# A layer's kernel with 128 series of products of zeros ahead of its first stage

## The chip, the cores and the metric

The kernel runs on one core of one Trainium2 chip. The metric is the device time of one execution in microseconds (us), lower is better. Two runs of the kernel before took 1088.96 and 1090.29 us; the median is 1089.62 us. One further execution was recorded by the hardware profiler. All rows of the profile come from that one.

## The reference

The reference computes one inference step of one layer (D = 1024) for a prompt of 512 tokens and a group of 8 x 8 sample tokens that share the weights. Cut to what matters here:

```python
u = _rms(x) * g_pre_mix
proj = u @ w_in                       # one projection: z, xbc, dt, q, k, v, gates, og
xbc, conv_new = causal_conv(xbc, conv_buf, conv_w, conv_b)
y_ssd, h_new = ssd_scan(silu(xbc) ...)          # 16 heads
h_ml, c_new, n_new, m_new = mlstm_scan(q, k, v, i_pre, logf, ...)   # 4 heads
x = x + _rms(concat(y_ssd, h_ml) @ w_out) * g_post_mix
x = x + _rms(cross_attention(_rms(x) * g_pre_x, mem_k, mem_v) @ w_xo) * g_post_x
f = (silu(u @ w_gate) * (u @ w_up)) @ w_down    # u = _rms(x) * g_pre_ffn
x = x + _rms(f) * g_post_ffn
```

All inputs and outputs are float32. Nothing in the reference answers to the products that the change adds: their operands are zeros, and nobody reads their result.

## The kernel before

The 576 tokens (512 of the prompt, 64 samples) lie along the free dimension of the tiles, the features along the 128 partitions, eight blocks of 128 deep. A float32 matrix product is made of three products of float32r parts: weights high by input high, weights high by input low, weights low by input high. Each part of the inputs is 576 columns wide and is taken in two pieces: 256 and 320 columns (`HALVES`) in the projections, 288 and 288 (`EHALVES`) in the output of the cross attention and in most of the feed-forward part. So a unit of weights, 128x1024, gives eight blocks, and per block and piece three products with 128x128 weights; each of them loads its weights anew (PEld in the profile) while the product ahead still runs.

Weights come by DMA in units of 512 KB into one of two `raw` buffers (L175). ScalarE copies the high part (L180), VectorE or a DMA on GpSimd's queue makes the low part (L184 to L187); there are three buffers for each of the split parts, so a later unit waits until TensorE is done with an earlier one.

The beginning: VectorE clears a small tile `wz` (L300), and TensorE makes 21 products of zeros with it, 256 columns of bfloat16 each, into the bank `ps_warm` (L303), which nobody reads. Meanwhile the input and the first two units of weights arrive in pieces on SP's queue (L304 to L314), ScalarE and VectorE make their high and low parts (L191, L192, L322, L323), and the first stage's products follow block by block (L339 to L341), then those of further units (`gemm`, L202 to L205).

Tiles are taken from pools. `MP` gives one of three PSUM banks by turns. `SL(n, ...)` gives one of the big slots of 576 x 8 floats for each partition; slot 1 has no user until the tile `qk` is made in a later part. Whoever takes a buffer waits for its last reader and writer.

Each engine works off its queue in order. In the first part of the kernel, up to the cross attention, the order of an engine's queue is chosen by a planner: it takes the order of the code as a priority, lets some pieces go earlier (`high_priority`) or behind others (`issue_after`), and goes by the times of a simulated run (`schedule_with_timeline_sim`). In the later part the order is written out by hand (`manual_schedule`, L2035 and L2238).

Of the kernel before, what the change touches and what calls it, by code (L numbers as in the profile page):

```python
# [11 lines left out]
F32 = mybir.dt.float32  # L12
F32R = mybir.dt.float32r
# [6 lines left out]
P = 128  # L20
# [95 lines left out]
def build(nc, tc, ctx, I, O):  # L116
    V, A, G, S, TE = nc.vector, nc.scalar, nc.gpsimd, nc.sync, nc.tensor
    mm = TE.matmul
# [12 lines left out]
    def SL(slot, name, dt=F32, shape=(P, KT, T)):  # L131

        return big.tile(list(shape), dt, name=name, tag="s%d" % slot, bufs=1)
# [5 lines left out]
    def MP(name="m"):  # L139
        return pa.tile([P, 512], F32, name=name, tag="a")  # L140
# [54 lines left out]
    def gemm(ps, units, xh, xl, t0, n, k0=0, k1=None, order=None, late=0):  # L195


        tiles = [(hi[:, j * P:(j + 1) * P], lo[:, j * P:(j + 1) * P]) for hi, lo, nk in units for j in range(nk)]
        order = order or range(len(tiles))
        for i, k in list(enumerate(order))[k0:k1]:  # L200
            (wh, wl), ah, al = tiles[k], xh(k, t0, n), xl(k, t0, n)
            mm(ps, wh, ah, start=i == 0, stop=False)  # L202
            mm(ps, wh, al, start=False, stop=False)  # L203
            for c in range(late) if i == late - 1 else [i] if i >= late else ():
                m = mm(ps, tiles[order[c]][1], xh(order[c], t0, n), start=False, stop=c == len(tiles) - 1)  # L205
        return m
# [94 lines left out]
    psw = MP("ps_warm")  # L301
    for _ in range(NWARM):
        mm(psw[:, 0:256], wz[:, 0:128], wz, start=True, stop=True, skip_group_check=True)  # L303
    S.dma_start(par, I["par"])  # L304

    wi = [[wp.tile([P, 1024], F32R, name=k, tag=k, bufs=3) for k in ("whi", "wlo")] for _ in range(2)]
# [46 lines left out]
    stop = gemm(ps0[2][1], [(*w2, KT)], U, UL, 256, 320, 0, NSS)  # L353
# [12 lines left out]
    stop = gemm(ps0[3][0], [(*w3, KT)], U, UL, 0, 256)  # L366
# [343 lines left out]
    for g in range(2):  # L710
        psb = BP("ps_ls")
        pb3 = psb.rearrange("p (h t) -> p h t", h=8)
        for h in range(8):
            mm(psb[:, h * TS:(h + 1) * TS], sel[:80, 8 * g + h:8 * g + h + 1].to_broadcast([80, P]), cumst[:, TP:T],
               start=h == 0, stop=h == 7, skip_group_check=True)
# [8 lines left out]
        for h in range(8):  # L724
            k, j = h % 2, (8 * g + h) // 2
            mm(psi[64 * k:64 * k + 64, j * TS:(j + 1) * TS], xdts[:, 8 * g + h, :], lm[:, h, :], start=True, stop=True,
               skip_group_check=True)
# [12 lines left out]
    for b in range(4):  # L740
# [3 lines left out]
        for g in range(2):  # L744
            for hb in (1, 0):
# [3 lines left out]
                   start=b == 0, stop=b == 3, skip_group_check=True)  # L749
# [139 lines left out]
    for h in range(4):  # L889
        q, k = qk[:, h, :], qk[:, 4 + h, :]  # L890
# [11 lines left out]
        for c in range(4):  # L902
            mm(pss[:, c * P:(c + 1) * P], k[:, c * P:(c + 1) * P], q[:, c * P:(c + 1) * P], start=True, stop=True,
               skip_group_check=True)
# [39 lines left out]
    for h in range(4):  # L944
        mm(psb[:, h * TS:(h + 1) * TS], sel[:68, h:h + 1].to_broadcast([68, P]), sxst[:, TP:T], start=h == 0, stop=h == 3,
           skip_group_check=True)
# [22 lines left out]
    for hb in range(2):  # L969
# [6 lines left out]
        for b in range(4):  # L976
# [3 lines left out]
            for h in range(4):  # L980
                mm(psn[32 * h:32 * h + 32, 0:257], qpad[:, h, bb, :], c0[:, h, 0:257], start=False, stop=b == 3,
                   skip_group_check=True)
# [241 lines left out]
    x = SL(1, "x1")  # L1224
# [956 lines left out]
    parts = [(c, d) for c in range(2) for d in range(2)]  # L2181
# [172 lines left out]
```

## Time and profile before

| | |
|---|---|
| median of two runs | 1089.62 us |
| the profiled execution's own time | 1087.01 us |
| its span, first to last instruction | 1085.2 us |
| mean granted TensorE clock | 0.998 of full speed |
| matrix products recorded | 8124 |
| TensorE products (PE) busy | 1075.0 us |
| TensorE weight loads (PEld) busy | 1022.1 us |
| VectorE (DVE) busy | 752.4 us |
| ScalarE (ACT) busy | 610.9 us |
| GpSimd (POOL) busy | 228.0 us |

Times in the profile count from the first instruction of the span. PE's records of neighbouring products overlap: a product is recorded from its start until its last column has left the array, so the time that a product takes from TensorE is the distance from its start to the next one's start, and not its recorded length. Weight loads overlap the product ahead. A row of the view of groups reads: line, engine, operation, output and inputs, weights' shape, moving operand's shape, count, then busy time in us, mean length in ns, and the idle time ahead with what ended it. In the order of time a row starts with start and length in us.

### The profile page before, as it was taken

How to read it: one execution, taken by the hardware profiler on the slowest of the kernel's cores; microseconds unless marked ns; L12 is line 12 of the kernel's file. 1: busy time of each engine (PE TensorE's matmuls, PEld its weight loads, DVE VectorE, ACT ScalarE, POOL GpSimd, SP SyncE). 2: the span in 40 equal slices, each digit the busy share in tenths (PEclk: the TensorE clock that was granted, in tenths of full speed). 3: DMA queues.
4: the chain of work that ended last, by engine and by line, in shares of the span. 5: the costliest groups of instructions: out<-in, count | busy, mean ns of one | idle time of the engine just before them, and what ended most of it. 6: DMA issues, size and time to landing. Idle time of an engine off the chain costs nothing.

```text
span 1085.2 us, 20708 instructions
## 1 busy us (share of the span) xinstructions
PE 1075.0 (99%) x8124; PEld 1022.1 (94%) x8124; DVE 752.4 (69%) x1507; ACT 610.9 (56%) x1098; POOL 228.0 (21%) x305
## 2 busy tenths in 40 slices
PE   9999999999999999999999999999999999999997
PEld 9999887778999999999999989999999999999997
DVE  6896785658877775568755546766467887787556
ACT  7867632355654555656555545645566566656653
POOL 1332643313113111000154301100011111111000
PEclk9999999999999999999999999999999999999999
DMA  6775535435654449653458775643486697578532
GB/s 211 179 159 126 161 111 172 165 80 185 190 152 144 110 123 324 226 193 101 152 194 288 271 252 180 239 133 92 135 176 137 159 203 163 117 189 184 125 131 88
DMA packets 58966, 182.29 MB, mean 168 GB/s; under 512 B 6604, under 2 KB 11852, under 8 KB 58356
## 3 DMA queue, kind: packets, MB, share of 16 engines
q1 hardware_dynamic: 42740, 138.06, 38.6%
q0 software_dynamic: 15552, 41.95, 19.6%
q8 instruction: 64, 1.05, 0.4%
q10 hardware_dynamic: 576, 0.95, 0.3%
q14 instruction: 34, 0.28, 0.1%
HBM read 160.28 MB, written 20.65 MB: 167 GB/s over the span
## 4 chain that ended last, share of the span: by engine, by line
PE 86%; DVE 5%; ACT 4%; issue 2%; DMA 2%; POOL 0%; DVEq 0%; SPq 0%; ACTq 0%; POOLq 0%
PE ps_in L203 4%; PE ps_in L202 4%; PE ps_in L205 4%; PE ps_v L815 3%; PE ps_o L205 3%; PE ps_o L203 3%; PE ps_g L1846 3%; PE ps_g L1847 3%; PE ps_o L202 3%; PE ps_u L1847 3%; PE ps_u L1848 3%; PE ps_u L1846 3%; PE ps_g L1848 3%; PE ps_dn L1846 2%; PE ps_dn L1847 2%
## 5 line engine op out<-in xcount | busy, mean ns | idle before, releaser
L202 PE MATMUL ps_in<-uh,whi 128*128 128x320 f32 (+1 forms) x544 | 162.9, 300 | 0.5 <-DVE cb L451 0.5
L205 PE MATMUL ps_in<-uh,wlo 128*128 128x320 f32 (+1 forms) x544 | 162.3, 299 | 0.3 <-DMA wlo<-win 0.3
L203 PE MATMUL ps_in<-ul,whi 128*128 128x320 f32 (+1 forms) x544 | 161.8, 298 | 0.0
L180 ACT CAST whi<-raw 128x1024 fp32r<-128x1024 f32 (+1 forms) x104 | 105.2, 1013 | 100.0 <-PE ps_in L203 25.9
L187 DVE TENSOR_TENSOR wlo<-raw,whi 128x512 fp32r<-128x512 f32 (+1 forms) x96 | 93.7, 978 | 75.1 <-ACT whi L180 74.0
L202 PEld LDWEIGHTS ps_in<-uh,whi 128*128 128x128 f32 x544 | 102.8, 189 | 3.3 <-issue 1.7
L205 PEld LDWEIGHTS ps_in<-uh,wlo 128*128 128x128 f32 x544 | 102.3, 188 | 1.5 <-DMA wlo<-win 0.5
L203 PEld LDWEIGHTS ps_in<-ul,whi 128*128 128x128 f32 x544 | 102.4, 188 | 0.6
L185 POOL DMA_DIRECT2D wlo<-win x32 | 27.8, 869 | 80.7 <-ACT wlo L184 70.0
L1847 PE MATMUL ps_g<-b,whi 128*128 128x288 f32 x144 | 42.5, 295 | 0.0
L1846 PE MATMUL ps_g<-b,whi 128*128 128x288 f32 x144 | 42.4, 295 | 0.0
L1847 PE MATMUL ps_u<-b,whi 128*128 128x288 f32 x144 | 42.4, 295 | 0.0
L1846 PE MATMUL ps_u<-b,whi 128*128 128x288 f32 x144 | 42.2, 294 | 0.0
L1819 ACT CAST whi<-rawx 128x1024 fp32r<-128x1024 f32 (+1 forms) x26 | 25.6, 984 | 27.9 <-PE ps_dn L1847 13.8
L192 DVE TENSOR_TENSOR wlo<-sw,whi 128x1024 fp32r<-128x1024 f32 (+1 forms) x26 | 29.6, 1140 | 14.9 <-ACT whi L191 14.8
L202 PE MATMUL ps_xo<-qh,whi 128*128 128x288 f32 x128 | 38.5, 303 | 0.2 <-ACT whi L180 0.2
L205 PE MATMUL ps_o<-mixm_h,wlo 128*128 128x256 f32 (+1 forms) x128 | 37.9, 296 | 0.0
L1798 ACT CAST whi<-raw 128x1024 fp32r<-128x1024 f32 (+1 forms) x26 | 25.6, 983 | 21.8 <-PE ps_g L1847 9.7
L203 PE MATMUL ps_xo<-ql,whi 128*128 128x288 f32 x128 | 37.8, 296 | 0.0
L205 PE MATMUL ps_o<-mixs_h,wlo 128*128 128x320 f32 (+1 forms) x128 | 37.7, 295 | 0.0
L203 PE MATMUL ps_o<-mixs_l,whi 128*128 128x320 f32 (+1 forms) x128 | 37.7, 295 | 0.0
L203 PE MATMUL ps_o<-mixm_l,whi 128*128 128x256 f32 (+1 forms) x128 | 37.7, 295 | 0.0
(769 smaller groups left out, 3853.6 us busy)
## 6 DMA issues: line engine op xcount, KB each, us to landing
raw<-win SPq DMA_DIRECT2D x35, 512.0 KB, 4.0
raw<-wout SPq DMA_DIRECT2D x17, 512.0 KB, 3.7
raw<-wxq SPq DMA_DIRECT2D x13, 512.0 KB, 6.0
raw<-wgate SPq DMA_DIRECT2D x13, 512.0 KB, 3.6
raw<-wup SPq DMA_DIRECT2D x13, 512.0 KB, 5.1
wlo<-win POOLq DMA_DIRECT2D x24, 256.0 KB, 5.1
kva<-vc SPq DMA_DIRECT2D x11, 512.0 KB, 5.0
raw<-wv SPq DMA_DIRECT2D x10, 512.0 KB, 4.0
```

The costliest lines, as they stand in the source:

```text
L180: casts.append(A.copy(hi[:, :n], raw[:, :n]))
L185: G.dma_start(lo[:, a:b], src[:, a:b], accum_op=ALU.add)
L187: e.tensor_tensor(lo[:, a:b], raw[:, a:b], hi[:, a:b].bitcast(F32), op=ALU.subtract)
L192: (eng or V).tensor_tensor(lo, src, hi.bitcast(F32), op=ALU.subtract)
L202: mm(ps, wh, ah, start=i == 0, stop=False)
L203: mm(ps, wh, al, start=False, stop=False)
L205: m = mm(ps, tiles[order[c]][1], xh(order[c], t0, n), start=False, stop=c == len(tiles) - 1)
L815: mm(ps, a, b, skip_group_check=True, **kw)
L1798: s.c1 = A.copy(s.h1[:, s.all], s.r1[:, s.all])
L1846: mm(ps, wh, b[0][k], start=start and k == 0, stop=False, skip_group_check=True)
L1847: mm(ps, wh, b[1][k], start=False, stop=False, skip_group_check=True)
L1848: m = mm(ps, wl, b[0][k], start=False, stop=k == nk - 1, skip_group_check=True)
```

## The change

Between the warm-up and the load of the parameters (`par`) come these lines. An array `bench` of 128 x 4608 zeros is made in slot 1 by one memset on VectorE. `SEG` gets two series for each of the 64 combinations of a, b and d: one with runs of 320, 256, 320, 256, 64, 256, 320 and 256 columns (12 products each, 2 of 64), one with 288, 64 and 288 columns (24, 2 and 24). The list is sorted by the number of runs, so all 64 series with 288 columns come first. Each product reads weights of 128x128 and some columns of the same array and writes one PSUM bank, `ps_probe`. The products go in threes: in the first, weights start at `w` and columns at `a`; in the second the columns start at `b` + 256; in the third the weights start 576 + `d` further on. a, b and d are 0, 16, 32 or 48 floats. TensorE keeps the order of the loop (`manual_schedule`). Nobody reads `ps_probe`, and nothing else of the kernel is changed.

```diff
@@ -301,6 +301,25 @@
     psw = MP("ps_warm")
     for _ in range(NWARM):
         mm(psw[:, 0:256], wz[:, 0:128], wz, start=True, stop=True, skip_group_check=True)
+
+    bench = SL(1, "bench", F32R, (P, 4608))
+    V.memset(bench.bitcast(F32), 0.0)
+    SEG = []
+    for a in (0, 16, 32, 48):
+        for b in (0, 16, 32, 48):
+            for d in (0, 16, 32, 48):
+                SEG.append((a, b, d, ((320, 12), (256, 12), (320, 12), (256, 12), (64, 2), (256, 12), (320, 12), (256, 12))))
+                SEG.append((a, b, d, ((288, 24), (64, 2), (288, 24))))
+    SEG.sort(key=lambda g: len(g[3]))
+    pq = MP("ps_probe")
+    with tc.manual_schedule(engines={TE.engine}):
+        for a, b, d, parts in SEG:
+            for n, count in parts:
+                for i in range(count):
+                    k = i // 3 % 4
+                    x = 64 + 576 * k + (b + 256 if i % 3 == 1 else a) + (256 if n == 320 else 0)
+                    w = 3200 + 128 * k + (d + 576 if i % 3 == 2 else 0)
+                    mm(pq[:, 0:n], bench[:, w:w + P], bench[:, x:x + n], start=i < 1, stop=True, skip_group_check=True)
     S.dma_start(par, I["par"])
```

## The prediction

> **What bounds the kernel now.** I read the top of the page first, then its clock row and the chain of work that ended last.
>
> ```profile
> span 1085.2 us, 20708 instructions
> PE 1075.0 (99%) x8124; PEld 1022.1 (94%) x8124; DVE 752.4 (69%) x1507; ACT 610.9 (56%) x1098; POOL 228.0 (21%) x305
> ...
> PEclk9999999999999999999999999999999999999999
> ...
> PE 86%; DVE 5%; ACT 4%; issue 2%; DMA 2%; POOL 0%; DVEq 0%; SPq 0%; ACTq 0%; POOLq 0%
> ```
>
> TensorE works in 1075.0 of 1085.2 us, has 86% of the chain, and runs at its full clock in all forty slices. So whatever is put into its queue is paid for. Only 10.2 us of the span are idle on it, and these are no room for new products: the stretch after 1060 us alone (below) holds 25.0 - 18.2 = 6.8 of them. It is an in-order engine, and the change puts its products ahead of everything but the warm-up. What matters, then, is how far apart two products start. A busy time can't tell that, because products overlap in the records; the count in a stretch can. The next rows are from the view of stretches (columns: stretch, length, busy time and count of PE, PEld, DVE, ACT and POOL, clock, DMA share, GB/s).
>
> ```profile
> 6.00:18.00 12.00, 12.00 (x91) 12.00 (x91) 9.74 (x18) 9.87 (x18) 0.91 (x3) 1.00 0.99 347
> 860.00:950.00 90.00, 90.00 (x682) 90.00 (x682) 70.15 (x134) 58.48 (x95) 14.84 (x18) 1.00 0.73 161
> 1000.00:1020.00 20.00, 20.00 (x153) 20.00 (x152) 12.29 (x24) 13.37 (x24) 2.55 (x3) 1.00 0.62 142
> 1040.00:1050.00 10.00, 10.00 (x70) 10.00 (x69) 6.16 (x12) 4.29 (x9) 0.00 (x0) 1.00 0.70 276
> 490.00:500.00 10.00, 10.00 (x87) 10.00 (x86) 10.00 (x23) 6.88 (x16) 0.00 (x0) 1.00 0.43 145
> 540.00:550.00 10.00, 10.00 (x88) 10.00 (x88) 4.66 (x11) 5.08 (x14) 4.64 (x3) 1.00 0.45 154
> ...
> 1060.00:1085.00 25.00, 18.21 (x154) 17.68 (x152) 15.30 (x31) 9.07 (x20) 0.00 (x0) 0.93 0.27 96
> ```
>
> Each of the five middle stretches holds products of one shape alone, 128x128 weights in float32r, as the groups of these stretches show: 288 columns in 860 to 950 and in 1000 to 1020, 320 in 1040 to 1050, 256 in 490 to 500 and in 540 to 550. A product is recorded for about 0.3 us, so two of each count began before the stretch; I take them off. That gives 90.00 / 680 = 132.4 ns and 20.00 / 151 = 132.5 ns for 288 columns, 10.00 / 68 = 147.1 ns for 320, and 10.00 / 85 = 117.6 and 10.00 / 86 = 116.3 ns for 256, of which I take 117.0. Per column that is 0.457 to 0.460 ns for all three. These are the three widths that the change adds.
>
> **The change part by part.** In the loops a, b and d take four values each: 64 combinations, with two series each, 128 series in all. Per combination one series has 36 products of 320 columns, 48 of 256 and 2 of 64, the other 48 of 288 and 2 of 64. That is 136 products, and 8704 in all, against 8124 recorded for the whole kernel of before. Nothing is removed.
>
> The long products, per combination: 36 x 147.1 = 5.296 us, 48 x 117.0 = 5.616 us, 48 x 132.4 = 6.355 us; together 17.267 us.
>
> The 64-column products: 4 per combination. No row shows this width in float32r with whole 128x128 weights. From above the nearest row is that of products with one column, where the weight load is all that is left to wait for:
>
> ```profile
> 23.52 1.17 PE L228 MATMUL ps_ss<-c,ssqx 128*128 128x1 f32 x10
> 24.55 0.39 PE L202 MATMUL ps_in<-uh,whi 128*128 128x320 f32 x1
> ```
>
> Ten of them start within 24.55 - 23.52 = 1.03 us: 103 ns each. From below stands the column rate, 64 x 0.46 = 29 ns. I take 103, since each of the 64-column products loads whole weights too: 0.412 us per combination; the other end would take 64 x 4 x 74 ns = 19 us off.
>
> So one combination costs 17.679 us, and 64 of them 1131.4 us. The series are sorted by their number of runs, so those of 288 columns come first: 64 x (6.355 + 0.206) = 420 us; the others follow with 64 x (5.296 + 5.616 + 0.206) = 712 us.
>
> The 64 distances are starts of the operands moved in steps of 16 floats, which is 64 bytes. What a distance costs can't be read by itself here. Operands do lie at many distances in the kernel: halves of 288 columns begin 1152 bytes apart, and in L1846 weights and moving columns even come out of one tile.
>
> ```profile
> 805.08 0.29 PE L1846 MATMUL ps_g<-u3h 128*128 128x288 f32 x1
> 805.21 0.30 PE L1847 MATMUL ps_g<-u3l,u3h 128*128 128x288 f32 x1
> 805.34 0.30 PE L1848 MATMUL ps_g<-u3h,wlo 128*128 128x288 f32 x1
> 805.47 0.29 PE L1846 MATMUL ps_g<-u3h,whi 128*128 128x288 f32 x1
> ```
>
> These three take 0.13 us from start to start like all others, so reading both from one tile, as the new products do, costs nothing by itself. The two stretches of 256 columns differ by 1.1%. As an estimate from them I allow 1.5% of the 1105 us of long products to either side for the mean over the distances: 17 us. [...]
>
> The memset of 128x4608 on VectorE comes ahead of the new products, and the first of them waits for it. Nothing else on TensorE can start meanwhile, but the warm-up does run.
>
> ```profile
> 0.84 0.17 DVE L300 MEMSET wz<- 128x128 uint32 x1 [0.84 <-PEq L2346]
> ...
> 1.06 4.66 PE L303 MATMUL ps_warm<-wz 128*128 128x256 bf16 x21 [1.06 <-DVE wz L300]
> 5.37 0.56 PE L339 MATMUL ps_in<-uh,whi 128*128 128x256 f32 x1
> ...
> L620 DVE COPY hs<-ps_h 128x512 f32<-128x512 f32 x2 | 1.4, 688 | 1.5 <-PE ps_h L616 1.5
> ```
>
> Bounds: by the copy, 4608 / 512 x 0.688 = 6.2 us; by the small memset, which took 0.17 us for 128, less than a fixed cost that can't be told apart, so anything from 1 us. It begins near 1.0 us and ends between 2 and 7.2; today's first real product starts at 5.37. The cost is 0 to 1.8 us; I take 0.5, for an end near 5.9. Queued behind it on VectorE is the splitting of the first input (L323, L192), whose reader is now more than 1100 us away: no cost.
>
> The first stage gains a little. All its inputs lie ready when the new products end, and the buffers for split weights are full. Today the stretch from 6 to 18 us holds 89 products of 256 and 320 columns in about equal parts, 134.8 ns each, where the rates above make 132.0: 89 x 2.8 ns = 0.2 us. With the slow start before it I take 1.2 us off; at most the idle time outside the tail, 10.2 - 6.8 = 3.4 us. The weights of later tiles are not further ahead than their three buffers, so the gain ends with the first tiles.
>
> The bank of the new products (one of three of that kind) and slot 1, which the array of zeros holds and the qk tile takes later, are free before their next user on the same in-order engine: no wait. But the order of the work up to the cross attention is made by a planner that times it, and it now sees 1.1 ms ahead of the first stage. It can order ACT's and VectorE's work there otherwise. I put nothing for it, and 8 us to either side, under 2% of that part; the rest is in an order written out by hand and can't change.
>
> The sum: 1131.4 + 0.5 - 1.2 = 1130.7 us. The profiled execution took 1087.0 us (the span of 1085.2 and 1.8 around it), so its time after is 2217.7. The median of the two timed runs, 1089.6, lies 2.6 above it; with that **2220 us**.
>
> **The rivals.** First, **a quieter machine**. The new products run while VectorE, ACT and the DMAs rest, whereas all rates above are from stretches where these work. If a part of each product is traffic in SBUF, it goes. The least per column that rows show is in products of 512 columns:
>
> ```profile
> 197.65 4.16 PE ps_v L815 x18
> ```
>
> 4.16 / 18 = 231 ns, and against 256 columns (231 - 117) / 256 = 0.445 ns for one more column. At that rate with nothing added a combination costs 36 x 142.4 + 48 x 113.9 + 48 x 128.2 ns + 0.412 us = 17.16 us, 64 make 1098, and the time is 2187. Against it: 288 columns took 132.4 ns with VectorE busy in 78% and the DMAs in 73%, and 132.5 with 61% and 62%; 256 took 117.6 with VectorE at 100% and 116.3 at 47%. Load on the other engines hardly moves the rate. [...]
>
> Second, **a load that shows**. If moving columns and the next weights get in each other's way at some distances, the weight load would no longer hide behind the product ahead. It is 103 ns by the one-column row. If this hits where the two starts are alike, a quarter of the combinations, 16 x 132 products x 103 ns = 217 us come on top: 2437. Against it: the products of L1846 above and the 94% of weight loading that hides in the whole kernel.
>
> Third, on the other side, **the products don't run**. Nothing reads the bank that they write, so a compiler or planner might drop them; the time would then be today's 1090, with perhaps the memset's microsecond. That decides from the first one dropped, since all have one form. Against it: the 21 products of L303 write a bank that nobody reads too, and they are in the trace.
>
> **How the numbers follow.** The forecast has 0.90, the quieter machine 0.05, the load that shows 0.04, dropped products 0.01. Around 2220 the parts reach 19 down (64 columns), 17 either way (distances) and 8 either way (planner); all at once is not likely, so the range goes from 2188, next to the quieter machine's 2187, to 2250. A change of under 2% could hardly be told from none here; all cases but the last lie 100% above. Faster by over 2% gets 0.005, within 2% 0.01, slower 0.985.
>
> **What would show it.** After: some 16800 products on PE; a first part near 420 us with 75 to 76 products in every 10 us, then 712 us in which runs of 320 and 256 alternate; granted clock full; other engines and DMA idle from some 25 us until 1137 us, and then the profile of before. A quieter machine shows as under 130 ns from start to start at 288 columns; a load that shows, as whole series that are slower than their neighbours; the planner, as other waits on TensorE between 1140 and 1650 us. I am wrong if the spacing differs from the three rates by more than 1.5%, or if the kernel's own part changes by over 8 us.

## The result, and the profile after

The changed kernel takes 2222.02 us (median of two runs, 2221.86 and 2222.18) against 1089.62: 2.041 times as long, with a 95% interval of 2.037 to 2.045. The forecast was 2220. The profiled execution took 2221.86 us, its span 2220.1; against the profiled one of before it is 1134.85 us longer.

The page of the changed kernel: its span, the engines' busy times, the slices of TensorE's clock and of the DMAs, the chain that ended last by engine, and one of its groups.

```profile
span 2220.1 us, 38121 instructions
PE 2209.6 (100%) x16828; PEld 2156.5 (97%) x16828; DVE 755.9 (34%) x1508; ACT 611.7 (28%) x1098; POOL 225.6 (10%) x305
...
PEclk9999999999999999999999999999999999999999
DMA  3000000000000000000008544654746864668673
...
PE 95%; DMA 1%; ACT 1%; issue 1%; DVE 1%; POOL 1%; DVEq 0%; ACTq 0%; POOLq 0%
...
L322 PE MATMUL ps_probe<-bench 128*128 128x288 f32 (+3 forms) x8704 | 1135.1, 293 | 0.0
```

All 8704 products ran: 16828 - 8704 = 8124 are left, as before. They took 1135.1 us without one idle moment ahead of them, and the granted clock, 0.999 in the mean, is at 9 (90% or more) in every slice. The busy times of the other engines are those of before to within 4 us; their share has halved because the span has doubled, and half of the DMAs' slices are empty. Of the old work only the first stage's splitting went under the new.

The changed kernel's stretches (columns as in the prediction) show the machine behind the first transfers, the part with 288 columns, and three samples of the part with 320 and 256:

```profile
25.00:1130.00 1105.00, 1105.00 (x8476) 1105.00 (x8475) 0.01 (x1) 0.00 (x0) 0.00 (x0) 1.00 0.00 1
110.00:410.00 300.00, 300.00 (x2282) 300.00 (x2281) 0.00 (x0) 0.00 (x0) 0.00 (x0) 1.00 0.00 1
440.00:540.00 100.00, 100.00 (x773) 100.00 (x772) 0.00 (x0) 0.00 (x0) 0.00 (x0) 1.00 0.00 1
740.00:840.00 100.00, 100.00 (x775) 100.00 (x774) 0.00 (x0) 0.00 (x0) 0.00 (x0) 1.00 0.00 1
940.00:1040.00 100.00, 100.00 (x771) 100.00 (x770) 0.00 (x0) 0.00 (x0) 0.00 (x0) 1.00 0.00 1
```

From 25 to 1130 us VectorE, ScalarE and GpSimd do next to nothing (0.01 us in all) and the DMAs rest. With the two taken off that began before the stretch, 2280 products start in 300 us: 76.0 in 10 us, as forecast. The counts of the three later samples, 771 to 775, are not equal: the series differ a little with the distance.

The beginning and the end of the new products, in the order of time (start and length in us first):

```profile
1.06 4.66 PE L303 MATMUL ps_warm<-wz 128*128 128x256 bf16 x21 [1.06 <-DVE wz L300]
5.68 0.98 PE L358 MATMUL ps_in<-uh,whi 128*128 128x256 f32 x3
6.50 1.74 PE L322 MATMUL ps_probe<-bench 128*128 128x288 f32 x12
...
1.91 3.90 DVE L306 MEMSET bench<- 128x4608 f32 x1 [0.91 <-issue]
...
1141.41 0.28 PE L359 MATMUL ps_in<-ul,whi 128*128 128x256 f32 x1
```

The memset ends at 5.81 us, and TensorE has used the wait: the planner put three products of the first stage (L358 is L339 of before) ahead of the new ones. These last from 6.50 to 1141.41 us: 1134.9 us. Taken one by one from the starts in the trace, the distance to the next start is:

| product | count | my term, ns | measured, ns | difference in all, us |
|---|---|---|---|---|
| 256 columns | 3072 | 117.0 | 117.9 | +2.6 |
| 288 columns | 3072 | 132.4 | 132.3 | -0.2 |
| 320 columns | 2304 | 147.1 | 146.6 | -1.2 |
| 64 columns | 256 | 103 | 112 | +2.3 |
| together | 8704 | 1131.4 us | 1134.9 us | +3.5 |

One thing in the order of the starts needs a word. Of two products of 64 columns the first has its successor 30 ns behind it in the mean, the second 110 ns, and the long product behind both takes 84 ns more than its like. The weight loads (PEld) fit this: behind such a pair they start 109 and 111 ns apart, one behind the other, and the product that comes next waits. In the table these 84 ns are counted with the pair: (30 + 110 + 84) / 2 = 112 ns.

### The profile page after: what moved, and what is told of

It is laid out like the page before. It is cut to its first block, busy times and chain, and to the rows that moved or that the text cites. A ratio compares the mean times of both kernels' runs of the same rounds, so it can differ in the third digit from the quotient of the medians.

```text
span 2220.1 us, 38121 instructions
## 1 busy us (share of the span) xinstructions
PE 2209.6 (100%) x16828; PEld 2156.5 (97%) x16828; DVE 755.9 (34%) x1508; ACT 611.7 (28%) x1098; POOL 225.6 (10%) x305
## 4 chain that ended last, share of the span: by engine, by line
PE 95%; DMA 1%; ACT 1%; issue 1%; DVE 1%; POOL 1%; DVEq 0%; ACTq 0%; POOLq 0%
PE ps_probe L322 51%; PE ps_in L203 3%; PE ps_in L202 3%; PE ps_in L205 3%; PE ps_v L834 2%; PE ps_o L205 2%; PE ps_o L203 2%; PE ps_g L1865 2%; PE ps_g L1866 2%; PE ps_o L202 2%; PE ps_u L1867 2%; PE ps_u L1866 2%; PE ps_g L1867 2%; PE ps_u L1865 2%; PE ps_dn L1865 1%; PE ps_dn L1866 1%
## 5 line engine op out<-in xcount | busy, mean ns | idle before, releaser
L322 PE MATMUL ps_probe<-bench 128*128 128x288 f32 (+3 forms) x8704 | 1135.1, 293 | 0.0
L322 PEld LDWEIGHTS ps_probe<-bench 128*128 128x128 f32 x8704 | 1135.0, 188 | 0.0
L180 ACT CAST whi<-raw 128x1024 fp32r<-128x1024 f32 (+1 forms) x104 | 105.4, 1014 | 107.9 <-PE ps_in L203 32.7
L239 POOL TENSOR_TENSOR rx_y<-rx_v,c 128x5 f32<-128x5 f32 x1 | 1.2, 1197 | 1135.1 <-DVE rx_v L238 1135.1
```

The source lines that it names most:

```text
L180: casts.append(A.copy(hi[:, :n], raw[:, :n]))
L239: pows.append(G.tensor_tensor(y, v, C32("nhalf")[:shape[0], :w], op=ALU.pow))
L322: mm(pq[:, 0:n], bench[:, w:w + P], bench[:, x:x + n], start=i < 1, stop=True, skip_group_check=True)
```

## The experiments

All are single executions of the changed kernel, with other new products, other contents of the array, or work added beside them. The kernel before took 1088.5 to 1088.7 us beside them.

**Half of the series.** The values of `a` are cut to two; the rest of the new products is left out.

```diff
-    for a in (0, 16, 32, 48):
+    for a in (0, 16):
```

> Half of the series: a takes 0 and 16 alone, so 32 combinations and 4352 products are left. My theory: the cost is the sum of the products' spacings, nothing else. The new products of the full change took 1134.9 us from the first start to the next stage's product, so half of them go with 567.5 us: about 1654 us, and the new products take 567 us from first to next. Rival: part of the cost is fixed (a lost order of the planner, a later start): then the time lies above 1654 by half of that part; with 20 us fixed it would be 1664.

Measured: 1654.3 us, and 566.9 us for the new products. The cost is additive. Twice 1654.3 less 2221.9 leaves 1086.7 us for everything but the series, and the kernel before alone took 1087.0 to 1090.3: no fixed part shows beyond this spread of 3 us, neither from the planner's other order nor from the start. The 64 series that both kernels have differ by 14 ns for the very first and by at most 4 ns for all others. So a series' time is not noise; something about it fixes it to a few nanoseconds.

**One distance.**

```diff
-                SEG.append((a, b, d, ((320, 12), ...
-                SEG.append((a, b, d, ((288, 24), ...
+                SEG.append((0, 0, 0, ((320, 12), ...
+                SEG.append((0, 0, 0, ((288, 24), ...
```

> All 128 series at the same distance, a = b = d = 0. In the full change the series of 256 and 320 columns took 10.96 to 11.31 us, those of 288 columns 6.51 to 6.63; the two at distance 0, 0, 0 took 11.251 and 6.533. Theory one: the addresses set a product's spacing to within a few per cent. Then all series are alike, within 0.02 us, and take 11.25 and 6.53 each: 64 x 17.784 = 1138 us, the time 2225. Theory two: the spread comes from elsewhere (when a series begins against the clocks, other traffic): then the series spread as before, 11.16 and 6.57 in the mean, and the time is 2222.

Measured: 2226.8 us, 1139.6 of them the new products. The stretches of this kernel:

```profile
110.00:410.00 300.00, 300.00 (x2294) 300.00 (x2293) 0.00 (x0) 0.00 (x0) 0.00 (x0) 1.00 0.00 1
440.00:540.00 100.00, 100.00 (x766) 100.00 (x765) 0.00 (x0) 0.00 (x0) 0.00 (x0) 1.00 0.00 1
740.00:840.00 100.00, 100.00 (x765) 100.00 (x765) 0.00 (x0) 0.00 (x0) 0.00 (x0) 1.00 0.00 1
```

Here the samples are equal, 766 and 765. All 64 series of 288 columns take 6.537 to 6.547 us, all others 11.252 to 11.260. Theory one holds: the addresses fix the time. At this distance 288 columns are a little quicker than in the mean of the change (6.575) and 256 and 320 a little slower (11.158). But it decides little: over all 64 distances the series lie between 10.96 and 11.31 us, 1.6% around the middle, and the mean for any one value of a, b or d is within 0.3% of the whole mean. Which of the starts fits which is not settled by these runs. What does follow is that the distances change single series, by up to 1.6%, and hardly their mean.

**Without the narrow products.** The 256 products of 64 columns are left out.

```diff
-                SEG.append((a, b, d, ((320, 12), (256, 12), (320, 12), (256, 12), (64, 2), (256, 12), (320, 12), (256, 12))))
-                SEG.append((a, b, d, ((288, 24), (64, 2), (288, 24))))
+                SEG.append((a, b, d, ((320, 12), (256, 12), (320, 12), (256, 12), (256, 12), (320, 12), (256, 12))))
+                SEG.append((a, b, d, ((288, 24), (288, 24))))
```

> The 256 products of 64 columns left out, the 8448 long ones kept. My theory: such a product costs one weight load, and a part of it is paid by the long product behind it, which took 84 us in 1000 more than its like, so 0.084 us more: (28 + 111 + 84) / 2 = 112 ns each, 28.7 us in all: 2193 us. By the term of my sum, 103 ns, it would be 26.4 us: 2196. Rival: they cost what stands between their own starts, 69.7 ns in the mean, and the 84 ns belong to the change of widths: then 17.8 us go, 2204, and the first long product of the second run still shows about 216 ns.

Measured: 2194.7 us, and 1106.5 us for the new products, 28.4 less than with them: 111 ns for each. No product of 288 columns takes over 145 ns any more. So the 84 ns behind a pair belong to the pair; a narrow product costs a weight load, and the term of 103 ns was 8% short. The whole time lies between my two values, 2193 and 2196, and a single execution can't tell these apart; the length of the new products can.

**A run of widths.** The series are replaced by runs of 48 products, and bfloat16 products come last.

```diff
+        for m in (128, 64, 32):
+            for n in (32, 64, 96, 128, 160, 192, 224, 256, 288, 320, 384, 448, 512):
+                for i in range(48):
...
+                    mm(pq[0:m, 0:n], bench[:, w:w + m], bench[:, x:x + n], start=True, stop=True, skip_group_check=True)
+        for n in (64, 128, 192, 256):
+            for i in range(48):
+                mm(pq[:, 0:n], wz[:, 0:128], wz[:, 0:n], start=True, stop=True, skip_group_check=True)
```

> The series replaced by runs of 48 products of one width, 32 to 512 columns, with weights of 128, 64 and 32 columns, and then by bfloat16 products of 64 to 256 columns with weights of 128. Theory one: spacing is the longer of the weight load (112 ns for 128 columns of weights) and the columns at 0.457 ns each. With 128 columns of weights: 112 ns up to 224 columns, 117 at 256, 132 at 288, 146 at 320, 231 at 512; with 64 and 32 columns of weights the floor falls to about 60 and 30 ns and the long ones stay at 132, 146 and 231. Theory two: what a long product takes above the bfloat16 rate is the weight load that reads beside it. Then 288 columns fall with narrower weights, from 132 to 127 and 124 ns or lower. In both: the whole time near 1335 us.

Measured: 1351.9 us. Stretches of this kernel, each inside runs of one form: 96 and 128 columns with 128 columns of weights; 288 columns with 128, with 64 and with 32 columns of weights; 256 columns in bfloat16.

```profile
25.00:42.00 17.00, 17.00 (x81) 17.00 (x81) 1.47 (x2) 0.57 (x1) 0.83 (x9) 0.50 0.00 1
73.00:78.00 5.00, 5.00 (x41) 5.00 (x40) 0.00 (x0) 0.00 (x0) 0.00 (x0) 1.00 0.00 0
148.00:153.00 5.00, 5.00 (x40) 5.00 (x39) 0.00 (x0) 0.00 (x0) 0.00 (x0) 1.00 0.00 0
217.00:222.00 5.00, 5.00 (x40) 4.12 (x39) 0.00 (x0) 0.00 (x0) 0.00 (x0) 1.00 0.00 0
267.00:271.00 4.00, 4.00 (x39) 3.60 (x37) 0.00 (x0) 0.00 (x0) 0.00 (x0) 1.00 0.00 0
```

From start to start the 288-column runs show 131.7, 130.0 and 131.1 ns. Narrower weights hardly help there, against the 127 and 124 ns of theory two. Theory one comes nearer, with floors of 112, 58 and 32 ns for 128, 64 and 32 columns of weights. At 256 columns, close above the floor, it misses too: the narrower weights bring 119.8 down to 113.3. The bfloat16 run has 109.2 ns at 256 columns, so at the one long width that ran in both types 6.5 of the 10.6 ns between them go with narrower weights, and what makes up the rest stays open. In bfloat16 no floor of 112 ns shows either: 64 columns took 29 ns with the same 128x128 weights loaded for each product.

The first row is what neither theory expected. The clock is 0.50, and the products from 64 to 160 columns stand 213 ns apart, though TensorE is busy all the time by its records. It happened once more, with 64 columns of weights: from 119.8 to 126.6 us the clock is at half again, and the products of 64 and 96 columns took 107 ns there, where 58 stood before. The whole took 17 us more than expected.

**Numbers in place of zeros.** The array is filled with the layer's input.

```diff
-    V.memset(bench.bitcast(F32), 0.0)
+    G.dma_start(bench.rearrange("p (k t) -> p k t", k=KT), I["xT"])
```

> The array is filled with the layer's input (random normal numbers) by one DMA instead of with zeros; all 8704 products as in the full change. My theory: the numbers don't matter; the series keep their times to the nanosecond (the first ones at 6.53 and 11.25 us), the new products take 1134.9 us, and the whole is 2222 us and at most 10 more for the later start. [...]

Measured: 2231.8 us. The first new product, in the order of time, and two stretches of this kernel:

```profile
11.41 3.01 PE L322 MATMUL ps_probe<-bench 128*128 128x288 f32 x11 [6.54 <-DMA bench<-xT]
```

```profile
0.00:20.00 20.00, 12.40 (x65) 11.24 (x66) 9.30 (x21) 10.09 (x20) 1.72 (x11) 0.74 0.93 339
20.00:420.00 400.00, 400.00 (x3044) 400.00 (x3043) 6.78 (x9) 6.22 (x9) 1.74 (x12) 1.00 0.01 4
```

The start is 4.9 us later (11.41 for 6.50), with TensorE idle for 6.54 us ahead of it. The granted clock is 0.74 in the mean of the first 20 us, which by an estimate from this figure is half the clock for some 10 of them, and the first series is 2.86 us longer; the second is 33 ns longer, all others are equal to those of zeros within 3 ns. Another 2.1 us of the longer time lie behind the new products, and what made them was not followed up. On this one core numbers cost what zeros cost, with a clock of 1.00 from 20 to 420 us.

**Narrow runs between long ones.** The series are replaced by the runs named in the expectation.

```diff
+        for m, n, count in ((128, 64, 6), (128, 64, 12), (128, 64, 24), (128, 64, 48), (128, 64, 96), (128, 128, 96),
+                            (128, 160, 96), (128, 192, 96), (128, 224, 96), (32, 32, 320), (32, 64, 320)):
+            for n_, count_, m_ in ((n, count, m), (288, 96, 128)):
...
```

> The series replaced by runs of narrow products, each followed by 96 products of 288 columns: 6, 12, 24, 48 and 96 products of 64 columns; 96 each of 128, 160, 192 and 224 columns, all with 128 columns of weights; and 320 each of 32 and 64 columns with 32 columns of weights. The run of widths showed 213 ns instead of 112 for 64 to 160 columns, at a granted clock of 0.51. Theory one: the clock halves when the array has been used too little for some microseconds, whatever the products' number. Then runs up to 24 products (2.7 us) stay at 112 ns, those of 96 (10.7 us) go over to 213 ns after 3 to 7 us, also for 128 columns; 192 and 224 columns, which use the array in over 70% of the 112 ns, stay at 112; and the 288-column run behind such a run starts at 240 ns and is back at 132 within some 5 us. The 64-column products with narrow weights stay at 32 ns. Time about 1340 us. Theory two: the half clock came from the run of 32 columns, or from the start, and once on full clock nothing falls: 112 ns throughout, about 1311 us.

Measured: 1320.9 us, between the two values named. The stretches around the run of 96 products of 64 columns, and those of 128 and 160 columns:

```profile
70.30:73.50 3.20, 3.20 (x31) 3.20 (x31) 0.00 (x0) 0.00 (x0) 0.00 (x0) 1.00 0.00 0
73.50:87.60 14.10, 14.10 (x68) 14.10 (x68) 0.00 (x0) 0.00 (x0) 0.00 (x0) 0.50 0.00 1
87.60:91.60 4.00, 4.00 (x21) 4.00 (x22) 0.00 (x0) 0.00 (x0) 0.00 (x0) 0.63 0.00 0
...
101.70:112.30 10.60, 10.60 (x97) 10.60 (x97) 0.00 (x0) 0.00 (x0) 0.00 (x0) 1.00 0.01 2
125.10:135.60 10.50, 10.50 (x96) 10.50 (x95) 0.00 (x0) 0.00 (x0) 0.00 (x0) 1.00 0.01 2
```

The busy share is 100% in all five; the clock is not. Runs of 6, 12 and 24 products stay at 112 ns. The run of 48 falls to 213 ns after 3.95 us, that of 96 after 3.29 us, and the 288 columns behind them need 3 to 4 us to come back. Theory two, that nothing falls from full clock, does not hold. Theory one does, but its time was 19 us too long and one of its numbers was wrong: 128 columns don't fall (111 ns throughout), nor do 160, nor the products with 32 columns of weights at 32 ns. From the half clock the run of widths didn't rise at 160 columns and did at 192: its clock is 0.50 from 20 to 50 us and 0.92 from 50 to 100, which by an estimate from these two figures puts the rise near 58. So the point of falling and the point of rising are not the same.

**Where it falls.** The same with 72 to 112 columns and a run of 256.

```diff
-        for m, n, count in ((128, 64, 6), (128, 64, 12), ...
+        for m, n, count in ((128, 72, 96), (128, 80, 96), (128, 88, 96), (128, 96, 96), (128, 104, 96), (128, 112, 96),
+                            (128, 256, 96)):
```

> Runs of 96 products of 72, 80, 88, 96, 104, 112 and 256 columns with 128 columns of weights, each behind 96 products of 288 columns on full clock. In the narrow runs 64 columns fell to the half clock after 3 to 4 us, 128 columns did not. Theory: it is decided by the share of time in which columns stream, columns x 0.457 ns over the 112 ns of a weight load: 26% at 64 columns fell, 52% at 128 did not, so there is one width between them from which on no run falls, and all narrower ones fall after 3 to 4 us. The times of a run of 96 are then 10.7 us above that width and about 17 us below it; I expect the change between 88 and 104 columns. Rival: the fall hangs on where the run begins against a fixed clock and not on the width; then the fallen ones are in no order of width.

Measured: 1278.6 us. The runs of 72, 80, 88 and 96 columns fell, after 4.98, 5.85, 3.39 and 6.08 us, and took 15.86, 15.02, 17.26 and 14.82 us; those of 104 and 112 didn't and took 10.66 each. Stretches around the runs of 88, 96 and 104:

```profile
65.00:81.00 16.00, 16.00 (x94) 16.00 (x93) 0.00 (x0) 0.00 (x0) 0.00 (x0) 0.63 0.00 1
96.00:112.00 16.00, 16.00 (x107) 16.00 (x106) 0.00 (x0) 0.00 (x0) 0.00 (x0) 0.73 0.00 0
126.00:142.00 16.00, 16.00 (x138) 16.00 (x138) 0.00 (x0) 0.00 (x0) 0.00 (x0) 1.00 0.00 1
```

Which runs fall goes in the order of width, as the theory has it. By the column rate, columns stream in 96 x 0.457 / 112 = 39% of the time where it still falls and in 42% where it doesn't. That it is the share and not the width fits the run of 32 columns with 32 columns of weights above: 32 x 0.457 / 32 = 46%, and it kept the full clock. The delay before the fall, 3.3 to 6.1 us, was expected at 3 to 4 and is in no order of width. Here the rival has its part: in the traces' records of the granted clock every stretch at one clock, but for the last of an execution, lasts a whole number of steps of 3.413 us (1, 2, 3, 4, 5, 14, 18, 315 and 647 of them among others; 1075.2 us before are 315, 2208.4 us of the changed kernel 647). Each of the six falls of these two runs comes at the end of the first step that lies in the narrow products, to within 0.2 us at its beginning. So in these runs the share of streaming decided whether the clock fell, and the place of the run on this grid decided when. The second fall of the run of widths agrees: the step that ends at 119.8 us holds 1.5 us of 32-column and 1.9 us of 64-column products with 64 columns of weights, 58 ns each, which makes 39% in the mean. It also says why 6, 12 and 24 products stayed at 112 ns: the longest of these runs took 2.6 us, less than one step.

**Other engines busy beside it.** Behind the new products' lines, for the first third of their time:

```diff
+    for _ in range(130):
+        A.copy(xs[:, 0:4, :], bench[:, 0:2304].bitcast(F32).rearrange("p (k t) -> p k t", k=4))
+        V.tensor_tensor(xs[:, 4:8, :], bench[:, 0:2304].bitcast(F32).rearrange("p (k t) -> p k t", k=4),
+                        bench[:, 2304:4608].bitcast(F32).rearrange("p (k t) -> p k t", k=4), op=ALU.add)
```

> The full change, and beside its products 130 times a copy of 128 x 2304 on ScalarE and an addition of two such operands on VectorE, both reading the array of zeros that TensorE reads: busy for some 350 us, then quiet. My theory: TensorE reads without sharing, so every series keeps its time to 0.02 us; the new products take 1134.9 us and the whole is 2222 us. The quieter machine (my first rival) expects the series beside the load to be longer: at the price that I gave, 3 to 4 ns for each product, 0.15 to 0.2 us for each of the first 50 series of 288 columns, some 8 to 10 us in all, with a step where the load ends.

Measured: 2220.8 us. A loaded and a quiet stretch of this kernel, and the same stretches of the changed kernel:

```profile
10.00:310.00 300.00, 300.00 (x2284) 300.00 (x2283) 296.42 (x134) 284.52 (x149) 28.55 (x12) 1.00 0.03 10
310.00:410.00 100.00, 100.00 (x762) 100.00 (x761) 46.01 (x18) 0.00 (x0) 0.00 (x0) 1.00 0.00 1
```

```profile
10.00:310.00 300.00, 300.00 (x2283) 300.00 (x2283) 11.82 (x18) 10.47 (x18) 1.73 (x12) 1.00 0.03 11
310.00:410.00 100.00, 100.00 (x762) 100.00 (x761) 0.00 (x0) 0.00 (x0) 0.00 (x0) 1.00 0.00 1
```

With VectorE busy in 99% and ScalarE in 95% of 300 us, reading the very array that TensorE reads, the products keep their places: the sum over all series differs by 6 ns, all of it in the first. For VectorE and ScalarE the first rival is done with, by this run more surely than by the comparison of stretches in the prediction. The DMAs rest here too (0.03 of their time, then none); that they don't lengthen a product rests on the rates alone, 132.4 ns at 288 columns with them busy in 73% and 132.3 without.

## Why the prediction was right, step by step

**The bound.** That TensorE's queue pays for all that is put in, and that the count of starts is what to read, held: 1135.1 us busy, no idle time, and half of the series cost half.

**The long products.** The three rates were read off stretches of 10 to 90 us and held for 1105 us to 0.7%, -0.1% and -0.4%. The allowance for the distances, 1.5% either way, was about the spread of single series (1.6%); their mean moved by less, and 1139.6 against 1134.9 us is what one distance for all would have cost.

**The narrow products.** The step "I take 103" was 9 ns short. The row of one-column products was the right one to go by, since both are bound by the weight load; but dividing 1.03 us by ten read it wrongly. In the trace of before the first of the ten has its successor 28 ns behind it, the nine others stand 111 to 112 ns apart, and the 320-column product behind them takes 228 ns instead of 147: the same pattern as at the 64-column pairs, with some 81 ns of the ten counted outside them. It cost 2.3 us.

**The start.** I gave the memset 0.5 us. It took 3.90 us and ended at 5.81, 0.1 before the time that I had chosen. The step that failed is "Nothing else on TensorE can start meanwhile": three products of the first stage did. Counted from the fourth of these (6.22 us before), the new ones begin 0.29 us late.

**The first stage's gain.** I took 1.2 us off, of which a row gave only 0.2. From the fourth product of the first stage to the last of the kernel it was 1071.72 us before and 1071.37 after: a gain of 0.35. It grew to 1.05 us within the first 110 us of the kernel's own work, but 0.6 us went again in the cross attention. TensorE's view of waits of the changed kernel (who waited for whom, us in total, times, longest) has one there that before doesn't have:

```profile
PE ps_os L1418 <- ACT kva L1443: 0.5, 1, 0.5
```

The inputs lying ready were worth about what I said; that the gain would last was the error. What made the new wait I didn't follow up. The 8 us allowed for the planner were not needed.

The sum in the terms of the profile: 1134.9 + 0.3 - 0.35 = 1134.85 us, which is the difference of the two profiled executions. Mine was 1130.7. The last 2.6 us that I added, for the distance of the median from the profiled run, weren't there after: this time the profiled run is itself one of the two runs, and the median lies 0.16 above it. So two errors of opposite sign, +4.15 and -2.4, make the good end look better than its parts.

**The rivals.** The quieter machine: 132.3 ns in silence against 132.4 in the working kernel, and no change under the load of VectorE and ScalarE. The load that shows: it shows where the product ahead is shorter than the load, at the 64-column pairs, which cost 28 us in all, and a little at 256 columns, where narrower weights saved 6.5 ns a product in the run of widths; at none of the 64 distances does a long series stand out by more than 1.6%. The 94% held against this rival is the share of the span in which weights are loaded, not of loads that are hidden; that products are busy in 99% beside it is what shows the overlap. Dropped products: all 8704 are there.

## What to carry to other kernels

On TensorE, busy in 99% of the span before, work put into the queue cost the sum of the distances between starts (1134.9 us, and the execution grew by 1134.85), and these can be read from the count of starts in a stretch of the same form: the forms carried over, to a per cent (0.7%, -0.1% and -0.4%), from a working kernel to an idle machine, and from numbers to zeros and back. Take the floor too: a float32r product with 128 columns of weights took 111 to 112 ns on the full clock at all widths run from 64 to 224 columns, and 118 at 256, so below about 224 narrower pieces bought nothing. And a long queue of such products of 96 columns or fewer was worse than its floor (96 products of 72 to 96 columns took 14.82 to 17.26 us, 96 of 104 columns 10.66): watch the granted clock, not the busy share.

## What the hardware showed that I had not expected

The clock fell to half (0.50) while TensorE was busy at 100% by its records. With 128 columns of weights in float32r, runs of 64 to 96 columns fell from 112 to 213 ns a product after 3.3 to 6.1 us, runs of 104 and more did not; once at half, the clock stayed there at 160 columns and came back at 192. In these traces the clock changed in steps of 3.413 us. What decided here was the share of time in which columns stream (it fell at 39% and below, and kept at 42% and above), not whether the queue had gaps.

The other surprise is how exact the machine is: with the same addresses in the same order, a series of 50 or 86 products took the same time to 4 ns in different kernels and executions, with zeros or numbers, with two engines loaded or at rest; only the first series of a run, or the first two behind the half clock, differ by more.
